# Feed-forward on split operands: the second token chunk's operands made inside the first chunk's product loop, three stage changes with new buffer pools, and the down stage's loads on three queues

## The chip, the core and the metric

The kernel runs on one core of one Trainium2 chip. A core has a matrix engine (TensorE; PE for its matmuls, PEld for its weight loads), VectorE (DVE), ScalarE (ACT), GpSimd (POOL), and SyncE (SP), which here only starts DMAs. Each engine works through its own instruction stream in order. ACT and POOL start DMAs too, and such a start stands in the same stream as their arithmetic. The metric is the device time of one execution in microseconds; lower is better.

## The reference, cut to what matters

With DEPTH = 1 there is one layer: 2-D neighbourhood attention with its residual, then a SwiGLU feed-forward with its residual, then a last norm. The same weights are applied to a prompt of 1024 tokens and a sample of 512 tokens.

```python
D_MODEL = 1024
D_FF = ((8 * D_MODEL // 3 + 255) // 256) * 256      # 2816

def rms_norm(x, g):
    y = xf * lax.rsqrt(jnp.mean(xf * xf, axis=-1, keepdims=True) + RMS_EPS)
    return (y * g.astype(jnp.float32)).astype(x.dtype)

def swiglu(x, w_gate, w_up, w_down):
    return (jax.nn.silu(x @ w_gate) * (x @ w_up)) @ w_down
...
        x = x + neighbourhood_attention(rms_norm(x, norm_mix[i]), ...)
        x = x + swiglu(rms_norm(x, norm_ffn[i]), ffn_w_gate[i], ffn_w_up[i], ffn_w_down[i])
    return rms_norm(x, norm_final)
```

All arrays are float32.

## The kernel before

**Numbers.** Each float32 operand of a matmul is split into a rounded part (a cast to fp32r on ACT, L135) and a remainder (a subtraction on DVE, L136). A product is three matmul passes: high by high, high by low, low by high (`PASS`). `split` does the two steps; ACT goes first and DVE waits for it.

**Feed-forward by seven products.** Gate, up and down are 2 x 2 block products done with seven half-size products in place of eight, so each side needs seven operands, some of which are sums and differences of blocks. The products run in the order 0, 1, 5, 4, 6, 2, 3, and some add to a PSUM bank from which ACT has meanwhile taken a copy (`blocks`, L758 to L783).

**Stages in question.**

1. *Output projection of the attention* (`project`, L575): token tiles of 128 rows. Each half row of x1 goes from the tile `xo` to DRAM (`x1_d`) by a store on POOL (L588).
2. *Norm and operands of the tokens* (`norm2`, L655, and `pair`, L669). The 12 tiles are two chunks of 6. `norm2` loads a tile of x1 (an ACT DMA, L658), forms the norm (square on ACT, power on POOL, multiplication by scale and gain on DVE, L119), transposes it on PE (L665) and copies it out of PSUM (ACT, L666). `pair` joins two tiles into seven operands. The first chunk's go to SBUF (`hops`), the second's to DRAM (`hop_d`) by SP stores (L684), and all six `norm2` of the second chunk are traced before the first product.
3. *Gate and up products* (`unit`, L785): chunk 0 with 11 column steps p, then chunk 1 with 11. A unit is 14 products of 12 matmuls (L751), seven for gate and seven for up. `w_raw` (L706) loads 512 KB of weights at a time on SP, two of five loads into the pool `rpool` that has been open from the start, three of five into `raw2` in the pool `fr`. `w_ops` makes the seven weight operands, tiles `wa`, `ws`, `wt`. The results of a unit go to DRAM as seven operands of the down product (`gop_d`, POOL stores, L802).
4. *Change of chunk* (L807 to L814): the operands of chunk 1 are loaded from `hop_d` in halves `hr` (SP, L812) and split into `hops2`, each into the buffer of chunk 0's operand of the same number.
5. *Down products* (L899 to L934): seven operands n, each with six token tiles tt of 33 matmuls (L907). `d_op` makes 11 weight tiles `wd` from 256 KB loads `dr` (SP, L831; sums on POOL, L845 to L854), `g_op` loads and splits `go` (SP, L861), `x_tile` loads x1 (SP, L873), `finish` norms and stores the result (power on POOL L886, scaling on DVE L889, store on SP, L890).

**What sets the order.** The program is traced in the order of the code. A scheduler then orders each engine's stream by which instruction it expects to be ready, with the trace order as priority. Pools lie in SBUF like two stacks, one from the left and one from the right; a pool opened after another was closed lies over its bytes, and a tile in it waits until the last reader of the bytes under it is done. With `reuse_waits="tile"` that is decided tile by tile.

Of the kernel before, what the change touches and what calls it, by code (L numbers as in the profile page):

```python
# [11 lines left out]
F32 = mybir.dt.float32  # L12
F32R = mybir.dt.float32r
# [42 lines left out]
def body(tc, xp, xs, g_mix, g_ffn, g_fin, w_qkv, rpb, w_o, w_g, w_u, w_d, yp, ys):  # L56
# [9 lines left out]
    with es:  # L66
# [22 lines left out]
        nc.gpsimd.memset(mhalf, -0.5)  # L89

# [539 lines left out]
        hop_cm, hop = pool("hop", bufs=1, reuse_waits="tile")  # L630

        def h_op(i):
            return hop.tile([P, 2, KB // 2, HT], F32R, tag=f"h{i}", name=f"h{i}")

        def operands(dst, xa, xb, tt):

            b11, b21, b12, b22 = xa[:, :4], xa[:, 4:], xb[:, :4], xb[:, 4:]
            t1, t2, t3, t4 = (tt[:, n] for n in range(4))
# [12 lines left out]
        n_cm, np_ = pool("npool", bufs=2, reuse_waits="tile")  # L651
        gb = np_.tile([P, D], F32, name="gbf", bufs=1)
        nc.sync.dma_start(out=gb, in_=bcast(g_ffn))

        def norm2(t):  # L655

            xn = np_.tile([P, D], F32, tag="xn", name="xn", bufs=3)
            nc.scalar.dma_start(out=xn, in_=x1_d[t * P:(t + 1) * P, :])  # L658
            xt = np_.tile([P, KB, P], F32, tag="xt", name="xt")
            rms(xn, gb, xn, xt.rearrange("p k t -> p (k t)"))  # L660
            for b in range(2):
                pt = psum("T", "pt")
                for kk in range(4):
                    k = b * 4 + kk
                    nc.tensor.transpose(pt[:, kk * P:(kk + 1) * P], xn[:, k * P:(k + 1) * P], ident)  # L665
                nc.scalar.copy(xt[:, b * 4:(b + 1) * 4], pt.rearrange("p (k t) -> p k t", k=4))  # L666
            return xt

        def pair(c, j, dst):  # L669
            xa = norm2(c * CT + j)  # L670
            xb = norm2(c * CT + 3 + j)
            tt = np_.tile([P, 4, KB // 2, P], F32, tag="tt", name="tt", bufs=1)
            operands(dst, xa, xb, tt)

        hops = [h_op(i) for i in range(7)]

        def to_sbuf(j):
            def dst(i, op):
                split(op, hops[i][:, 0, :, j * P:(j + 1) * P], hops[i][:, 1, :, j * P:(j + 1) * P])
            return dst  # L680

        def to_dram(j):
            def dst(i, op):
                nc.sync.dma_start(out=hop_d[i, :, :, j * P:(j + 1) * P], in_=op)  # L684
            return dst

        chores = Chores([oh_job(t) for t in range(TP // P - 1, NT)])
        for j in range(3):
            chores.do()
            drain(ofill)  # L690
            pair(0, j, to_sbuf(j))
# [7 lines left out]
        n_cm.__exit__(None, None, None)  # L699
# [3 lines left out]
        fr_cm, fr = pool("fr", bufs=1, side="right", reuse_waits="tile")  # L703
        turn = [0]

        def w_raw(src):  # L706
            turn[0] += 1
            r = rpool.tile([P, 1024], F32, tag="raw", name="wr") if turn[0] % 5 < 2 else \
                fr.tile([P, 1024], F32, tag="raw2", name="wr", bufs=3)
            v = r.rearrange("p (k f) -> p k f", k=KB // 2)  # L710
            nc.sync.dma_start(out=v, in_=src.rearrange("(k p) f -> p k f", p=P))
            return v

        def w_ops(w, p):
# [5 lines left out]
            def one(a):  # L720
                o = fr.tile([P, 2, KB // 2, P], F32R, tag="wa", name="wa", bufs=6)
                split(a, o[:, 0], o[:, 1])
                return lambda z, k: o[:, z, k]

            def two(s):
                o = fr.tile([P, 2, 2, KB // 2, P], F32R, tag="ws", name="ws", bufs=3)
                split(s.rearrange("p s k f -> p (s k f)"), o[:, 0].rearrange("p s k f -> p (s k f)"),
                      o[:, 1].rearrange("p s k f -> p (s k f)"))
                return [lambda z, k, n=n: o[:, z, n, k] for n in range(2)]

            def sums():
                return fr.tile([P, 2, KB // 2, P], F32, tag="wt", name="wt", bufs=3)
# [12 lines left out]
            ops[3] = one(a22)  # L745
# [59 lines left out]
        for p in range(NP):  # L805
            unit(0, p, hops)
        hops2 = [None] * 7  # L807
        for i in (0, 1, 5, 4, 6, 2, 3):
            o = h_op(i)
            for k in range(0, KB // 2, 2):  # L810
                r = fr.tile([P, 2, HT], F32, tag="hr", name="hr", bufs=3)
# [5 lines left out]
        fr_cm.__exit__(None, None, None)  # L817
        fl_cm.__exit__(None, None, None)
        hop_cm.__exit__(None, None, None)
        r_cm.__exit__(None, None, None)  # L820


        dr_cm, drp = pool("drp", bufs=1, side="right", reuse_waits="tile")
        dl_cm, dl = pool("dl", bufs=1, reuse_waits="tile")
        gf = dl.tile([P, D], F32, name="gff")
        nc.sync.dma_start(out=gf, in_=bcast(g_fin))

        def d_raw(i, f, d):
            r = dl.tile([P, 512], F32, tag="dr", name="dr", bufs=6)
            row = (2 * i + f) * P  # L830
            nc.sync.dma_start(out=r, in_=w_d[row:row + P, d * 512:(d + 1) * 512])  # L831
            return r
# [3 lines left out]
        def d_op(n, i):  # L836
# [18 lines left out]
            o = drp.tile([P, 2, 512], F32R, tag="wd", name="wd", bufs=17)  # L855
# [3 lines left out]
        def g_op(n, tt):  # L859
            r = dl.tile([P, NP, P], F32, tag="gr", name="gr", bufs=2)  # L860
# [15 lines left out]
        def finish(t, xs):  # L876
# [10 lines left out]
            for n, (x, y) in enumerate(zip(xs, ys_)):  # L887
                hs = slice(n * 512, (n + 1) * 512)
                nc.vector.scalar_tensor_tensor(y, x, rs, gf[:, hs], ALU.mult, ALU.mult)  # L889
                nc.sync.dma_start(out=yrow(t)[:, hs], in_=y)  # L890
# [8 lines left out]
        for n in (0, 1, 4, 5, 2, 6, 3):  # L899
            wds = [d_op(n, i) for i in range(NP)]  # L900
            for tt in range(6):
# [33 lines left out]
        dl_cm.__exit__(None, None, None)  # L935
        dr_cm.__exit__(None, None, None)
# [17 lines left out]
```

## Time and profile before

| | |
|---|---|
| median of three runs | 1861.57 us (1859.36 to 1862.14) |
| the profiled execution's own time | 1861.16 us |
| its span, first to last instruction | 1859.4 us |
| mean granted TensorE clock | 0.986 |
| PE busy | 1764.7 us, 95% |
| DVE, ACT, POOL busy | 64%, 47%, 24% |
| matmuls of L751 (gate and up) | 3696 |
| matmuls of L907 (down) | 1386 |

Between the span and the profiled execution's own time lie 1.8 us, and between that and the median 0.4 us. PE's matmuls are pipelined, so their listed duration is longer than the step from one to the next; how long PE stood still is read from the idle time in front of a matmul, which the profile gives with what ended it. The stages lie in the span as follows: attention and projection to 812.1 us, gate and up of chunk 0 to 1163.05, of chunk 1 to 1490.44, down products from there to 1851.2, and the last norm and stores to the end.

### The profile page before, as it was taken

To read this page: it belongs to the slowest core of one execution; us is meant where nothing else is said; L and a number is where in the kernel's file an instruction comes from. 1 tells how busy PE (TensorE), PEld (TensorE's weight loads), DVE (VectorE), ACT (ScalarE), POOL (GpSimd) and SP (SyncE) were. 2 spreads that over 40 slices of the span, in tenths; PEclk is the share of its full clock that TensorE was granted. 3 is DMA by queue.
4 is the path that set the end of the run, shared out by engine and by line. 5 is a ranking of instruction groups with operands and counts; after the bars stand their busy time and mean duration, and the time that the engine had idled before them with its cause. 6 is when DMAs were issued, how large, how long until landed. Compare 5 with 4: busy or idle time off the path is not lost.

```text
span 1859.4 us, 25647 instructions
## 1 busy us (share of the span) xinstructions
PE 1764.7 (95%) x9178; PEld 1520.4 (82%) x9178; DVE 1192.7 (64%) x2191; ACT 864.8 (47%) x1706; POOL 447.3 (24%) x494
## 2 busy tenths in 40 slices
PE   8999999999989999988999999999999969999898
PEld 6887777777767777868999999899999958787676
DVE  4401877777886566668777777877777444556554
ACT  4412766666885455544443444544344333333322
POOL 1211000000130000112243342424334224425510
PEclk9999999999999999989999999999999989999999
DMA  7755444333464442776333434534343187545632
GB/s 243 224 176 160 111 111 109 101 102 101 127 203 143 128 145 94 224 242 190 111 119 117 135 113 153 162 118 124 107 131 103 58 304 241 202 133 190 220 122 99
DMA packets 222047, 278.79 MB, mean 150 GB/s; under 512 B 25600, under 2 KB 171776, under 8 KB 221920
## 3 DMA queue, kind: packets, MB, share of 16 engines
q1 hardware_dynamic: 201824, 210.69, 37.6%
q0 software_dynamic: 18368, 60.18, 9.5%
q10 hardware_dynamic: 1728, 6.29, 1.1%
q8 instruction: 72, 1.18, 0.3%
q14 instruction: 55, 0.45, 0.1%
HBM read 213.20 MB, written 76.43 MB: 156 GB/s over the span
## 4 chain that ended last, share of the span: by engine, by line
PE 67%; DVE 11%; DMA 10%; ACT 6%; issue 3%; SPq 2%; POOL 2%; DVEq 0%; POOLq 0%; ACTq 0%
PE pa L751 19%; PE pd L907 13%; PE pd L751 9%; PE pgv L275 7%; DMA vr<-v_d 5%; PE pg L329 5%; PE pb L751 5%; PE pgo L583 4%; DVE pT L421 2%; SPq L375 2%; DMA dr<-ffn_w_down 1%; ACT s L402 1%; PE pss L391 1%; PE ptt L417 1%; PE po L428 1%
## 5 line engine op out<-in xcount | busy, mean ns | idle before, releaser
L907 PE MATMUL pd<-wd,go 128*128 128x512 f32 x1386 | 331.0, 400 | 29.8 <-ACT go L135 19.3
L907 PEld LDWEIGHTS pd<-wd,go 128*128 128x128 f32 x1386 | 262.4, 190 | 98.3 <-ACT go L135 20.3
L751 PE MATMUL pa<-h,ws 128*128 128x384 f32 x1056 | 201.5, 340 | 2.8 <-ACT c L774 2.0
L751 PE MATMUL pa<-h,wa 128*128 128x384 f32 x1056 | 194.1, 339 | 7.4 <-ACT wa L135 5.1
L751 PE MATMUL pd<-h,ws 128*128 128x384 f32 x1056 | 198.6, 337 | 1.5 <-ACT h L135 0.9
L329 PE MATMUL pg<-hTp,whl 128*128 128x512 f32 x768 | 197.0, 403 | 0.0
L751 PEld LDWEIGHTS pa<-h,wa 128*128 128x128 f32 x1056 | 184.9, 190 | 9.2 <-ACT wa L135 5.6
L751 PEld LDWEIGHTS pa<-h,ws 128*128 128x128 f32 x1056 | 184.6, 190 | 6.7 <-ACT c L774 5.3
L136 DVE TENSOR_TENSOR ws<-wt,ws 128x1024 fp32r<-128x1024 f32 x88 | 108.5, 1234 | 126.5 <-ACT ws L135 126.3
L751 PEld LDWEIGHTS pd<-h,ws 128*128 128x128 f32 x1056 | 184.7, 188 | 2.1 <-ACT h L135 1.2
L329 PEld LDWEIGHTS pg<-hTp,whl 128*128 128x128 f32 x768 | 140.2, 189 | 29.8 <-issue 0.4
L802 POOL DMA_DIRECT2D gop_d<-c x66 | 50.5, 765 | 386.9 <-DVE c L793 379.7
L402 ACT ACTIVATE s<-s,mx 128x384 f32<-128x384 f32 (+1 forms) x192 | 110.7, 580 | 66.5 <-DVE mx L399 66.2
L583 PE MATMUL pgo<-wo,oh 128*128 128x512 f32 x576 | 139.3, 392 | 0.0
L136 DVE TENSOR_TENSOR wa<-wr,wa 128x512 fp32r<-128x512 f32 x132 | 117.9, 897 | 18.8 <-ACT wa L135 18.2
L135 ACT CAST ws<-wt 128x1024 fp32r<-128x1024 f32 x88 | 92.5, 1052 | 68.5 <-PE pd L751 65.3
L583 PEld LDWEIGHTS pgo<-wo,oh 128*128 128x128 f32 x576 | 105.5, 188 | 20.6 <-DVE oh L136 0.3
L135 ACT CAST go<-gr 128x1408 fp32r<-128x1408 f32 x42 | 57.7, 1373 | 138.4 <-PE pd L907 116.7
L135 ACT CAST wa<-wr 128x512 fp32r<-128x512 f32 x132 | 81.4, 621 | 63.3 <-PE pb L751 40.0
L751 PE MATMUL pb<-h,wa 128*128 128x384 f32 x528 | 101.8, 342 | 3.6 <-DVE c L771 3.6
L421 DVE TENSOR_TENSOR pT<-ptt,pT 128x384 fp32r<-128x384 f32 (+1 forms) x192 | 90.0, 507 | 21.2 <-ACT pT L420 20.5
L329 PE MATMUL pg<-hTs,whl 128*128 128x512 f32 x384 | 102.6, 404 | 0.8 <-DVE q L340 0.8
(137 smaller groups left out, 2859.0 us busy)
## 6 DMA issues: line engine op xcount, KB each, us to landing
gr<-gop_d SPq DMA_DIRECT2D x42, 704.0 KB
dr<-ffn_w_down SPq DMA_DIRECT2D x99, 256.0 KB
wr<-ffn_w_gate SPq DMA_DIRECT2D x44, 512.0 KB
wr<-ffn_w_up SPq DMA_DIRECT2D x44, 512.0 KB
wr<-na_w_qkv SPq DMA_DIRECT2D x38, 512.0 KB
gop_d<-gs POOLq DMA_DIRECT2D x88, 192.0 KB, 4.3
gop_d<-c POOLq DMA_DIRECT2D x66, 192.0 KB, 2.8
vr<-v_d SPq DMA_DIRECT2D x192, 64.0 KB
```

The lines of the kernel that those rows point to most:

```text
L135: nc.scalar.copy(hi, raw)
L136: nc.vector.tensor_tensor(lo, raw, f32(hi), ALU.subtract)
L275: nc.tensor.matmul(pg, hh[a][:, k, c:c + P], wv[k // 2][b][:, k % 2], start=(k == 0 and i == 0), stop=(k == KB - 1 and i == 2))
L329: nc.tensor.matmul(pg, w[:, a, k, :], h[b][:, k, c:c + 512], start=(k == 0 and i == 0), stop=(k == KB - 1 and i == 2))
L375: nc.sync.dma_start(out=raw[:, j * P:(j + 1) * P], in_=src[:, BS[j]:BS[j] + 32, :])
L391: nc.tensor.matmul(pt[:, :n], q[h * HD:(h + 1) * HD, a, j].rearrange("p r i -> p (r i)"), kv[:, krow:krow + nrow, BS[j]:BS[j] + 32], start ...
L402: nc.scalar.activation(s[:, :n], s[:, :n], AF.Exp, bias=mx, scale=-1.0, accum_out=sm)
L421: nc.vector.tensor_tensor(pT[:, :n, 1], pv, f32(pT[:, :n, 0]), ALU.subtract)
L583: nc.tensor.matmul(pg, ohs[k // 4][:, a, k % 4], wo[:, b, k, n * 512:(n + 1) * 512], start=(k == 0 and i == 0), stop=(k == KB - 1 and i == 2))
L751: nc.tensor.matmul(bank[:, :HT], a(y, k), b[:, z, k], start=start and k == 0 and i == 0, stop=k == KB // 2 - 1 and i == 2, skip_group_chec ...
L802: nc.gpsimd.dma_start(out=gop_d[i, 3 * c:3 * c + 3, :, p].rearrange("j q t -> q j t"), in_=a.rearrange("q (j t) -> q j t", j=3))
L907: nc.tensor.matmul(pd, go[:, y, i], wds[i][:, z], start=(i == 0 and m == 0), stop=(i == NP - 1 and m == 2))
```

## The change

The second chunk's operands are made between the first chunk's units, `pair1` behind units 2, 4 and 6. The gain of the norm, a broadcast tile of 512 KB (`gb`), becomes a tile `gT` with one column for each block of 128 features, loaded at the start of the kernel, and is multiplied in where the transposed tile leaves PSUM: that copy moves from ACT to DVE, and the scaling of the row from DVE to ACT. Chunk 0's operands lie in `hop` in the order of use, so the reload of chunk 1 goes one buffer down: operand number n in the order goes where number n - 1 lay, and the first goes to a pool of its own, `hx`, traced ahead of the last unit. The weight operand tiles move from the right stack to the left (`fa`, over the closed norm pool) and are fewer: `wa` 6 before, now 2 in `fa` and 2 for the last operand in `a2p`; `ws` and `wt` 3 before, now 2 each. The reload's halves and `pair1`'s tiles share four 4 KB buffers (`t4p`); `pair1`'s x1 tiles take turns with the weight loads in `raw2`.

In the down stage `wd` lies left, the `gr`, `dr` and `go` buffers right. `dr` has 4 buffers where it had 6, `go` one in each of two pools, `g1p` first. The load of `gr` goes to ACT's queue, x1 loads and the first half of the result's stores to POOL's, and `dr` loads and the other stores stay on SP.

```diff
+        gT = cpool.tile([P, KB], F32, name="gT")
+        nc.sync.dma_start(out=gT, in_=g_ffn.rearrange("(k p) -> p k", p=P))
...
+        ORDER = (0, 1, 5, 4, 6, 2, 3)
...
-        def norm2(t):
+        def norm2(t, xn, xt):
...
-            rms(xn, gb, xn, xt.rearrange("p k t -> p (k t)"))
+            nc.scalar.activation(xt.rearrange("p k t -> p (k t)"), xn, AF.Square, accum_out=ms)
...
+            nc.gpsimd.tensor_tensor(rs, me, mhalf, ALU.pow)
+            nc.scalar.mul(xn, xn, rs)
...
-                nc.scalar.copy(xt[:, b * 4:(b + 1) * 4], pt.rearrange("p (k t) -> p k t", k=4))
+                nc.vector.tensor_tensor(xt[:, ks], pt.rearrange("p (k t) -> p k t", k=4),
+                                        gT[:, ks].rearrange("p (k o) -> p k o", o=1).to_broadcast([P, 4, P]),
+                                        ALU.mult)
...
+        n_cm.__exit__(None, None, None)
+        fa_cm, fa = pool("fa", bufs=2, reuse_waits="tile")
...
-        for j in range(3):
-            pair(1, j, to_dram(j))
...
-        fr_cm, fr = pool("fr", bufs=1, side="right", reuse_waits="tile")
+        t4_cm, t4p = pool("t4p", bufs=4, side="right", reuse_waits="tile")
+        r2_cm, r2p = pool("r2p", bufs=3, side="right", reuse_waits="tile")
+        a2_cm, a2p = pool("a2p", bufs=2, side="right", reuse_waits="tile")
+        hx_cm, hx = pool("hx", bufs=1, side="right", reuse_waits="tile")
...
+        def pair1(j):
+            xs = []
+            for t in (CT + j, CT + 3 + j):
+                xn = r2p.tile([P, 1024], F32, tag="raw2", name="xn")
+                xt = temp().rearrange("p (k t) -> p k t", k=KB)
+                norm2(t, xn, xt)
+                xs.append(xt)
+            tt = [temp().rearrange("p (s k t) -> p s k t", s=2, k=KB // 2) for _ in range(2)]
+
+            def dst(i, op):
+                nc.sync.dma_start(out=hop_d[i, :, :, j * P:(j + 1) * P], in_=op)
+            operands(dst, *xs, [tt[n // 2][:, n % 2] for n in range(4)])
...
+        def reload(n):
+
+            i = ORDER[n]
+            o = h_op(n - 1) if n else h_op("x", hx)
+            for k in range(0, KB // 2, 2):
+                r = temp()[:, :2 * HT].rearrange("p (k t) -> p k t", k=2)
+                nc.sync.dma_start(out=r, in_=hop_d[i, :, k:k + 2])
+                split(r, o[:, 0, k:k + 2], o[:, 1, k:k + 2])
+            hops2[i] = o
+
+        for p in range(NP):
+            unit(0, p, hops)
+            if p in (2, 4, 6):
+                pair1(p // 2 - 1)
+            if p == NP - 2:
+                reload(0)
+        for n in range(1, 7):
+            reload(n)
...
-        dr_cm, drp = pool("drp", bufs=1, side="right", reuse_waits="tile")
+        gr_cm, grp = pool("grp", bufs=2, side="right", reuse_waits="tile")
+        g0_cm, g0p = pool("g0p", bufs=1, side="right", reuse_waits="tile")
+        dr_cm, drp = pool("drp", bufs=4, side="right", reuse_waits="tile")
+        g1_cm, g1p = pool("g1p", bufs=1, side="right", reuse_waits="tile")
+        wd_cm, wdp = pool("wdp", bufs=17, reuse_waits="tile")
         dl_cm, dl = pool("dl", bufs=1, reuse_waits="tile")
+        turn = [0]
...
-            nc.sync.dma_start(out=r, in_=gop_d[n, tt])
-            o = dl.tile([P, 2, NP, P], F32R, tag="go", name="go", bufs=2)
+            nc.scalar.dma_start(out=r, in_=gop_d[n, tt])
+            turn[0] += 1
+            o = (g0p, g1p)[turn[0] % 2].tile([P, 2, NP, P], F32R, tag="go", name="go")
...
-            nc.sync.dma_start(out=x, in_=x1_d[t * P:(t + 1) * P, d * 512:(d + 1) * 512])
+            nc.gpsimd.dma_start(out=x, in_=x1_d[t * P:(t + 1) * P, d * 512:(d + 1) * 512])
...
-                nc.sync.dma_start(out=yrow(t)[:, hs], in_=y)
+                queue.dma_start(out=yrow(t)[:, hs], in_=y)
...
-                    finish(rows(tt, 0), (c11[tt], c12[tt]))
+                    finish(rows(tt, 0), (c11[tt], c12[tt]), nc.gpsimd)
...
-                    finish(rows(tt, 1), (u2[tt], c22[tt]))
+                    finish(rows(tt, 1), (u2[tt], c22[tt]), nc.sync)
```

More of the change, by code (lines that the diff above doesn't have):

```diff
@@ L630, in body, with h_op @@
         hop_cm, hop = pool("hop", bufs=1, reuse_waits="tile")
-        def h_op(i):
-            return hop.tile([P, 2, KB // 2, HT], F32R, tag=f"h{i}", name=f"h{i}")
+        ORDER = (0, 1, 5, 4, 6, 2, 3)
+        def h_op(n, where=None):
+            return (where or hop).tile([P, 2, KB // 2, HT], F32R, tag=f"h{n}", name=f"h{n}")
         def operands(dst, xa, xb, tt):
             b11, b21, b12, b22 = xa[:, :4], xa[:, 4:], xb[:, :4], xb[:, 4:]
-            t1, t2, t3, t4 = (tt[:, n] for n in range(4))
+            t1, t2, t3, t4 = tt
             dst(0, b11)
@@ L718, in w_ops, with one @@
             a11, a21, a12, a22 = d1[:, :, :P], d1[:, :, P:], d2[:, :, :P], d2[:, :, P:]
-            def one(a):
-                o = fr.tile([P, 2, KB // 2, P], F32R, tag="wa", name="wa", bufs=6)
+            def one(a, where=fa):
+                o = where.tile([P, 2, KB // 2, P], F32R, tag="wa", name="wa")
                 split(a, o[:, 0], o[:, 1])
@@ L744, in w_ops @@
             ops[6], ops[2] = two(r)
-            ops[3] = one(a22)
+            ops[3] = one(a22, a2p)
             return ops
@@ L828, in d_raw @@
         def d_raw(i, f, d):
-            r = dl.tile([P, 512], F32, tag="dr", name="dr", bufs=6)
+            r = drp.tile([P, 512], F32, tag="dr", name="dr")
             row = (2 * i + f) * P
```

64 lines of the change are left out of this document (29 added, 35 removed).

## The prediction

> **What bounds the kernel now.** The page's span and chain come first.
>
> ```profile
> span 1859.4 us, 25647 instructions
> ...
> PE 67%; DVE 11%; DMA 10%; ACT 6%; issue 3%; SPq 2%; POOL 2%; DVEq 0%; POOLq 0%; ACTq 0%
> ```
>
> The chain that ends last is mostly PE, so a change pays only where PE stands still. The view of busy time by stretches, cut at the stage changes, tells where that is. Columns: start:end, length, PE, PEld, DVE, ACT, POOL busy (instructions), granted clock, DMA share, GB/s.
>
> ```profile
> 812.10:863.10 51.00, 36.33 (x176) 32.97 (x175) 35.65 (x53) 25.30 (x43) 3.69 (x5) 0.80 0.84 260
> 863.10:1163.05 299.95, 299.95 (x1724) 297.85 (x1723) 225.95 (x297) 129.11 (x213) 107.36 (x112) 1.00 0.42 126
> 1163.05:1181.50 18.45, 13.90 (x74) 12.43 (x74) 15.46 (x19) 11.39 (x18) 9.27 (x9) 1.00 0.79 250
> 1181.50:1490.44 308.94, 308.93 (x1775) 307.18 (x1775) 214.92 (x284) 123.28 (x204) 107.39 (x113) 1.00 0.35 106
> 1490.44:1508.73 18.29, 1.22 (x2) 0.50 (x2) 10.06 (x13) 8.78 (x13) 6.88 (x9) 0.59 0.95 341
> 1508.73:1689.80 181.07, 180.75 (x769) 144.95 (x770) 88.04 (x85) 59.43 (x74) 63.34 (x41) 0.99 0.60 203
> 1689.80:1772.90 83.10, 70.65 (x289) 54.20 (x287) 55.28 (x60) 30.60 (x51) 44.09 (x32) 0.98 0.67 218
> 1772.90:1851.20 78.30, 78.30 (x328) 62.71 (x328) 35.04 (x44) 20.01 (x33) 7.80 (x8) 0.98 0.31 108
> ```
>
> Inside the units PE is full; it stands still at the three stage changes and in one stretch of the down stage. What a stage would take without stalls comes from the chain in order of time (the same point of two units, nine units apart) and the DVE timeline (PSUM read after two successive tiles).
>
> ```profile
> 1196.16 4.16 PE pa L751 x24
> ...
> 1459.23 4.16 PE pa L751 x24
> ```
>
> ```profile
> 1789.67 0.69 DVE L893 TENSOR_TENSOR c<-c,pd 128x512 f32<-128x512 f32 x1 [4.67 <-PE pd L907]
> ...
> 1797.37 0.69 DVE L893 TENSOR_TENSOR c<-c,pd 128x512 f32<-128x512 f32 x1 [4.66 <-PE pd L907]
> ```
>
> A unit takes 263.07 / 9 = 29.23 us, 11 units 321.5; a down tile 7.70, 42 tiles 323.4. The ledger: chunk 0 takes 350.95 (812.10 to 1163.05), 29.4 too much. Chunk 1 takes 327.4, 5.9 too much. The down products take 360.8 (1490.44 to 1851.20), 37.4 too much: 17.8 before they run, 83.10 - 289/33 x 7.70 = 15.7 in the stretch from 1689.80, and 3.9 elsewhere.
>
> **First change, 812 us.** PE and ACT timelines, SP timeline, a stretch, and two groups:
>
> ```profile
> 819.36 3.33 PE L751 MATMUL pa<-h,wa 128*128 128x384 f32 x9 [4.91 <-ACT wa L135]
> 825.72 1.94 PE L665 MATMUL pt<-ident,xn 128*128 128x128 f32 x8 [3.03 <-DVE xn L119]
> ```
>
> ```profile
> 818.69 0.62 ACT L135 CAST wa<-wr 128x512 fp32r<-128x512 f32 x1 [3.56 <-DMA x_d<-xo]
> ...
> 822.48 1.14 ACT L135 CAST wa<-wr 128x512 fp32r<-128x512 f32 x2 [0.28 <-DMA wr<-ffn_w_gate]
> ```
>
> ```profile
> 814.66 1.47 SPq L711 DMA_DIRECT2D wr<-ffn_w_gate  x1
> ```
>
> ```profile
> 820.20:832.00 11.80, 8.77 (x32) 8.26 (x32) 8.14 (x12) 5.54 (x9) 1.42 (x2) 0.52 1.03 321
> ```
>
> ```profile
> L119 DVE SCALAR_TENSOR_TENSOR xn<-xn,rs,gbf 128x1024 f32<-128x1024 f32 x12 | 15.4, 1285 | 8.4 <-POOL rs L116 8.4
> L665 PE MATMUL pt<-ident,xn 128*128 128x128 f32 x96 | 13.7, 289 | 4.1 <-DVE xn L119 3.7 <-ACT xt L666 0.3
> L666 ACT COPY xt<-pt 128x512 f32<-128x512 f32 x24 | 13.0, 591 | 17.4 <-PE pt L665 17.4
> ```
>
> The first `wa` lies over the projection's `xo` and waits for its store (3.56). The change puts `wa` over the norm pool, done before 812, so product 0 can follow the projection at once. The second load still lies over `wo`, read to 812.1; its operands are late next. A 512 KB load took 4.56 us in an empty pipe (x at the start, below) and 7.8 here beside stores (814.66 to 822.48). With 0.62 for the cast and less the 2.08 of product 0 (half of the 4.16 for 24 matmuls), PE waits 3.1 to 6.4; I take 3.5, near the empty pipe, since the stores of the second chunk are gone from there. The half clock (0.52 for 11.8 us) behind a wait of 4.91 cost up to 5.7; I take 2.5. The transposes stay PE work, at most 13.7 / 2 = 6.9, so 29.4 - 6.9 = 22.5 is stall, and **16.5** goes (10.4 to 19.4). The Trainium skill, "TensorE: Matmul & The Clock Gate", Part 1, states that an idle window of some 3.4 us throttles the array; the row with 4.91 agrees; by it, 3.1 of idle would keep the clock and the sum gains 2.5.
>
> The norm itself: per tile ACT gives two copies of 0.591 for one full-width scaling (the nearest row, DVE's, is 1.285), DVE gives 1.285 for two PSUM reads of 0.69. That is nothing on PE. In the units DVE is 75% busy (225.95 of 299.95), which hides it; without that cover it would be about 1.4 us a tile.
>
> **The second chunk among the units.** Each `norm2` puts an ACT DMA that waits for a `raw2` buffer, two ACT passes, and PE transposes that wait for them into full streams; behind the ACT wait stand PSUM copies that PE needs; behind the seven SP stores of a pair, weight loads, which run ahead. Nothing shows this; the nearest row is the transposes' 3.03. Six tiles cost 0 to 18.2; I take 0.7 each, because the DMA share is 0.42 there and was 1.03 around that row: **-4**.
>
> **Second change, 1163 us.** PE timeline, ACT timeline, group:
>
> ```profile
> 1173.49 2.36 PE L751 MATMUL pa<-h,ws 128*128 128x384 f32 x12 [1.96 <-ACT c L774]
> ```
>
> ```profile
> 1176.93 0.83 ACT L135 CAST h<-hr 128x768 fp32r<-128x768 f32 x1 [3.11 <-DMA hr<-hop_d]
> ```
>
> ```profile
> L136 DVE TENSOR_TENSOR h<-hr,h 128x768 fp32r<-128x768 f32 x14 | 14.2, 1025 | 4.8 <-ACT h L135 4.8
> ```
>
> One buffer down gives each operand one product (2.08 us) more, and operand 0 (2 x 1.025 of DVE) goes ahead. Twelve halves are still 12.3 us of DVE within two blocks in which it is mostly busy. Of 5.9 I take **3.5** (0 to 5.9).
>
> **Third change, 1490 us.** SP's waits; PE, ACT, DVE timeline:
>
> ```profile
> SPq L831 <- PE pa L751: 51.3, 1, 51.3
> ```
>
> ```profile
> 1505.65 1.36 ACT L135 CAST go<-gr 128x1408 fp32r<-128x1408 f32 x1 [1.14 <-DMA gr<-gop_d]
> 1507.05 1.63 DVE L136 TENSOR_TENSOR go<-gr,go 128x1408 fp32r<-128x1408 f32 x1 [1.82 <-ACT go L135]
> ...
> 1507.07 1.22 PE L907 MATMUL pd<-wd,go 128*128 128x512 f32 x2 [16.64 <-ACT go L135]
> ```
>
> SP waits 51.3 us for the last product, since `dr` lies over its operand; then come 11 loads, then `gr`. In the new layout `wd` 0 to 10 lie over `rpool` and operands used early in the last block, `dr` and `gr` over closed temporaries: all can be there at the end. What is late next is `go`: `g1p`, taken first, lies over `a2p`, which the last product reads. PE then waits 1.36 + 1.63 and a little, 3.2; I add 1 for late `wd`. 17.8 - 4.2 = **13.6** goes (0 to 14.6; 0 if SP, in order, is held by the load of `gff`, which now lies over that last operand).
>
> **Fourth, 1690 to 1773 us.** SP's and PE's waits in this stretch, the one after it, and a group:
>
> ```profile
> SPq L890 <- DVE yo L889: 30.3, 12, 6.4
> ```
>
> ```profile
> PE pd L907 <- DVE go L136: 9.7, 6, 4.1
> ```
>
> ```profile
> 1772.90:1782.00 9.10, 9.10 (x32) 7.25 (x33) 2.70 (x4) 0.03 (x1) 5.05 (x3) 0.81 0.48 159
> ```
>
> ```profile
> L802 POOL DMA_DIRECT2D gop_d<-gs x88 | 67.3, 767 | 0.1
> ```
>
> SP stands 30.3 us before result stores, with `dr` loads queued behind; weights come late and hold ACT, DVE, and `go`. The stores go to POOL, which here works 44.09 of 83.10; 12 stores and 6 x1 loads add 18 x 0.767 = 13.8, and behind each store's wait for L889 stand the weight sums for the next operand. The `gr` loads now wait in ACT's stream for DVE's remainder of an earlier tile, in front of `wd` casts; ACT, busy 30.60 of 83.10, has room for that. And `dr` has 4 buffers, not 6. So I take half of 15.7 and 1 of the clock's 3.9 (0.81 after the last wait): **9** (-5 to 19.6). The Trainium skill, "DMA: Bandwidth & Descriptors", section "Issuing engines are not separate DMA queues", states that issuing from several engines saves only sequencer time; the DMA share of 0.67 does not contradict it, but SP's 30.3 us show that order can matter.
>
> **Start.** Timelines of SP and ACT:
>
> ```profile
> 0.74 0.38 SPq L246 DMA_DIRECT2D x<-x_prompt  x1
> ...
> 5.30 1.06 ACT L112 ACTIVATE xn<-x 128x1024 f32<-128x1024 f32 x1 [3.28 <-DMA x<-x_prompt]
> ...
> 18.55 3.98 SPq L305 DMA_DIRECT2D t_d<-na_rpb  x6
> ```
>
> `gT` is traced before the first x load, on which everything waits: 1024 pieces of 4 bytes. A table load of 240 pieces takes SP 3.98 / 6 = 0.66; by pieces that is 2.8. I take **-3** (0 to -5).
>
> **Sum:** 16.5 - 4 + 3.5 + 13.6 + 9 - 3 = 35.6 less than the profiled execution's 1861.2, which is 0.4 under the median: **1826 us**. All good ends give 1802, all bad ones 1879.
>
> **Rivals.**
> - *The down stage starts late as before* (SP held by `gff`, or `gr` by the last `gop_d` stores). For it: SP's 51.3 us wait. Against: SP's timeline shows weight loads (L711) started 23 us ahead of stores traced earlier (L684), so what isn't ready need not hold the rest.
>
> ```profile
> 790.02 0.38 SPq L711 DMA_DIRECT2D wr<-ffn_w_gate  x1
> ...
> 813.28 1.27 SPq L684 DMA_DIRECT2D hop_d<-xt  x2
> ```
>
>   1826 + 13.6 = 1840. Chance 0.12.
> - *Other queues win nothing in the fourth stretch*: either transfers share engines, as the page says, or POOL becomes what SP was. 1826 + 9 = 1835, to 1840. Chance 0.15; it lies inside the range.
> - *Slower:* the units lose. A copy on ACT must be done within one product:
>
> ```profile
> 1025.21 2.03 PEld L751 LDWEIGHTS pa<-h,ws 128*128 128x128 f32 x12 [0.16 <-ACT c L774]
> ```
>
>   There is 0.16 us of stall already. With `ws` 2 and `wa` 2 + 2, a cast that waits for a product in front of that copy holds PE. From 35.6 / 22 = 1.6 us a unit the gain is gone; at 2 us the time is 1870. Against: by the code a `ws` buffer is read last by the fourth of seven products and needed again by the third of the next seven, five products or 10.4 us on. Chance 0.13.
> - *Nothing in sum:* the stalls move, 1861. Chance 0.05.
>
> **Chances and range.** My forecast has 0.55 (1808 to 1842). The range 1808 to 1852 leaves out the slower rival, the null and tails, 0.2. A measurement tells 0.2%, 3.7 us, from no change: faster 0.81, same 0.05, slower 0.14.
>
> **What would show it.** First change: `wa` cast before 812, one PE wait of 3 to 6 us. Units: L751 with some 4 us of idle; over 20 speaks for the slower rival. 1163: under 3 us. Third: L907 starts within 5 us of the last L751. Fourth: no SP wait before stores, and POOL's own waits for DVE `yo` under 15 us. First ACT square near 8.3 us rather than 5.30. I am wrong if unit periods exceed 30 us, or if L907 starts 15 us late.

## The result and the profile after

| | before | after |
|---|---|---|
| median of four runs each, one chip | 1860.46 us (1856.5 to 1862.14) | 1874.99 us (1874.36 to 1877.8) |
| ratio, 95% interval | | 1.0082 (1.0065 to 1.01) |
| the profiled execution's own time, its span | 1861.16, 1859.4 us | 1877.8, 1875.7 us |
| chunk 0 of gate and up (321.5 us without stalls) | 350.95 | 359.7 |
| chunk 1 (321.5) | 327.4 | 326.0 |
| down products (323.4) | 360.8 | 369.7 |

The change makes the kernel slower by 14.5 us. The prediction said 1826 us, 1808 to 1852; the time lies above the range, on the slower side, which had a chance of 0.14.

Lines have moved: L751 is now L775, L907 is L945, `dr` loads L868, `gr` L898, x1 loads L911, powers L664 and L924, weight sums of the down stage L882 to L891. The view of busy time by stretches of the changed kernel, cut as the prediction's was (start:end, length, PE, PEld, DVE, ACT, POOL busy, clock, DMA share, GB/s):

```profile
812.70:845.42 32.72, 29.18 (x157) 28.54 (x156) 22.81 (x34) 15.50 (x24) 1.31 (x2) 0.95 0.52 159
845.42:1172.39 326.97, 307.76 (x1742) 301.77 (x1741) 232.43 (x321) 141.26 (x229) 107.79 (x117) 0.98 0.47 145
1172.39:1190.00 17.61, 16.07 (x90) 15.43 (x90) 16.55 (x20) 10.04 (x18) 9.78 (x9) 1.00 0.83 280
1190.00:1498.40 308.40, 307.22 (x1760) 306.13 (x1759) 220.13 (x288) 124.29 (x205) 107.18 (x113) 1.00 0.36 110
1498.40:1531.70 33.30, 21.53 (x69) 15.30 (x69) 13.83 (x17) 11.70 (x17) 17.94 (x27) 0.85 0.92 317
1531.70:1726.50 194.80, 188.51 (x790) 150.21 (x790) 95.01 (x92) 59.50 (x75) 75.43 (x49) 0.98 0.52 173
1726.50:1791.17 64.67, 52.38 (x201) 39.97 (x200) 36.17 (x46) 24.23 (x43) 37.66 (x39) 0.92 0.69 227
1791.17:1868.10 76.93, 76.93 (x328) 61.41 (x328) 40.08 (x47) 21.37 (x34) 11.69 (x10) 1.00 0.34 115
```

Compare it with the table of before. PE was full from 863 to 1163 us, with not one stall inside the units; now it stands still for 326.97 - 307.76 = 19.2 us there and runs at a lower clock behind the longer waits. The start of the down stage still has a hole, and so has the stretch in which the first half of the result is finished. The first boundary is what did come out. PE timeline:

```profile
817.87 0.62 PE L775 MATMUL pb<-h,wa 128*128 128x384 f32 x2 [2.93 <-ACT wa L137]
819.09 3.01 PE L775 MATMUL pb<-h,wa 128*128 128x384 f32 x10 [0.60 <-DVE wa L138]
```

Two waits of 2.93 and 0.60 us stand where there was a stall of 22.5. By 845.42 the matmuls are 5.6 us behind an unbroken stream.

**Where the time went.** Chunk 0 lasts 8.7 us longer (the units lost more than the boundary gained), chunk 1 is 1.4 shorter, the down stage 8.9 longer; with 0.6 more before and 0.6 less behind, that is the 16.3 us between the spans. Code that is the same everywhere spreads as well: the projection ends between 806.9 and 812.7 us in the profiles of this study, and chunk 0 with unchanged code took 355 to 360.5 us. So what follows compares stages, and takes the timed ratios for the whole.

**In the units.** The largest of PE's waits and of SP's from 812 to 1173 us (total, times, longest), then the timelines of SP, ACT, POOL, ACT and PE before the longest wait:

```profile
PE pa L775 <- ACT c L793: 7.3, 3, 4.7
PE pa L775 <- ACT c L798: 5.9, 4, 4.9
PE pb L775 <- ACT wa L137: 5.2, 3, 2.9
PE pd L775 <- ACT c L801: 2.3, 2, 1.6
```

```profile
SPq L735 <- DVE wa L138: 186.0, 27, 17.3
SPq L735 <- PE pt L671: 41.1, 3, 22.0
SPq L735 <- DVE me L662: 22.0, 1, 22.0
```

```profile
911.39 8.99 SPq L727 DMA_DIRECT2D hop_d<-t  x7
920.47 2.64 SPq L735 DMA_DIRECT2D wr<-ffn_w_gate  x2
```

```profile
942.26 1.06 ACT L660 ACTIVATE t<-xn 128x1024 f32<-128x1024 f32 x1 [0.50 <-DMA xn<-x_d]
```

```profile
945.22 1.92 POOL L821 TENSOR_TENSOR gs<-c 128x384 f32<-128x384 f32 x1 [0.66 <-DVE c L817]
...
955.11 1.08 POOL L664 TENSOR_TENSOR rs<-me,mhalf 128x1 f32<-128x1 f32 x2
```

```profile
955.71 1.15 ACT L665 ACTIVATE xn<-xn,rs 128x1024 f32<-128x1024 f32 x1 [5.37 <-POOL rs L664]
...
958.22 0.46 ACT L798 COPY c<-pa 128x384 f32<-128x384 f32 x1
```

```profile
958.73 4.21 PE L775 MATMUL pa<-h,ws 128*128 128x384 f32 x12 [4.88 <-ACT c L798]
```

Read from the bottom: PE waits for ACT's copy of a PSUM bank. In ACT's stream the scaling of `xn` stands before that copy and waits for the power; POOL reaches the power only at 955.11, behind a unit's sums and stores. It is so late because the tile's x1 came late (squares at 940 to 943). The rows of SP's waits explain more than this one wait: for 41.1 + 22.0 us SP's weight loads wait for a transpose (L671) or a statistic (L662) of the pair. The pair's two x1 tiles take turns in the three `raw2` buffers, and the weights that should be loaded there, and SP's queue behind them, wait until `xn` is read.

### The profile page after: what moved, and what is told of

The parts are those of the page before. It is cut to its first block, busy times and chain, and to the rows that moved or that the text cites. A ratio compares the mean times of both kernels' runs of the same rounds, so it can differ in the third digit from the quotient of the medians.

```text
span 1875.7 us, 25644 instructions
## 1 busy us (share of the span) xinstructions
PE 1775.9 (95%) x9178; PEld 1528.7 (82%) x9178; DVE 1187.4 (63%) x2203; ACT 863.8 (46%) x1694; POOL 466.7 (25%) x530
## 5 line engine op out<-in xcount | busy, mean ns | idle before, releaser
L945 PE MATMUL pd<-wd,go 128*128 128x512 f32 x1386 | 339.3, 406 | 30.3 <-DVE go L138 13.2
L945 PEld LDWEIGHTS pd<-wd,go 128*128 128x128 f32 x1386 | 266.9, 194 | 102.7 <-DVE go L138 16.8
L775 PE MATMUL pa<-h,ws 128*128 128x384 f32 x1056 | 202.7, 340 | 16.4 <-ACT c L798 8.4
L775 PEld LDWEIGHTS pa<-h,ws 128*128 128x128 f32 x1056 | 186.5, 191 | 20.7 <-ACT c L798 10.3
L775 PE MATMUL pd<-h,ws 128*128 128x384 f32 x1056 | 198.4, 335 | 2.3 <-ACT c L801 2.3
L775 PEld LDWEIGHTS pd<-h,ws 128*128 128x128 f32 x1056 | 184.9, 188 | 3.0 <-ACT c L801 3.0
L775 PE MATMUL pa<-h,wa 128*128 128x384 f32 x792 | 149.2, 338 | 0.8 <-DVE c L803 0.8
L775 PEld LDWEIGHTS pa<-h,wa 128*128 128x128 f32 x792 | 139.4, 188 | 1.9 <-DVE c L803 1.8
L775 PE MATMUL pb<-h,wa 128*128 128x384 f32 x528 | 100.8, 338 | 6.0 <-ACT wa L137 5.2
```

What stands on the lines that cost most here:

```text
L775: nc.tensor.matmul(bank[:, :HT], a(y, k), b[:, z, k], start=start and k == 0 and i == 0, stop=k == KB // 2 - 1 and i == 2, skip_group_chec ...
L945: nc.tensor.matmul(pd, go[:, y, i], wds[i][:, z], start=(i == 0 and m == 0), stop=(i == NP - 1 and m == 2))
```

## The experiments

"Against before" is the difference of the medians on the same chip, with the ratio's interval; the changed kernel itself stands at +14.5 us (1.0065 to 1.01). "Loss" is the length of a stage less its time without stalls. Each diff is against the changed kernel unless said otherwise.

**1. The `dr` buffers off the last product's operand.** By the built program's addresses the first `dr` buffer lies at 194 to 196 KB of each partition, inside `a2p`'s second buffer (192 to 196 KB), which holds the operand of the very last gate and up product. Opened ahead of `g0p`, `dr` lies at 205 to 213 KB.

```diff
-        g0_cm, g0p = pool("g0p", bufs=1, ...)
         dr_cm, drp = pool("drp", bufs=4, ...)
+        g0_cm, g0p = pool("g0p", bufs=1, ...)
```

> Changed kernel with the pools of dr and of the second go tile opened in the other order, so that the four dr buffers lie over weight-load and temporary bytes that are free before the last product. Theory (the dr loads, in order on SP, are held by the buffer that the last product reads): loads start before the last product ends, the start of the down stage loses 5 to 8 us in place of 17.2, and the time falls by 9 to 13, to 1862 to 1866. Rival (the start is bound by the go tile over the same kind of buffer, or by the 11 casts themselves): the loss stays above 14 and the time within 3 of 1875.

Measured: 1867.75 us, 8.8 against before (1.0032 to 1.0065). SP's queue (timeline), the changed kernel first, then this run:

```profile
1498.45 5.47 SPq L868 DMA_DIRECT2D dr<-ffn_w_down  x5
```

```profile
1467.50 28.95 SPq L868 DMA_DIRECT2D dr<-ffn_w_down  x8
```

The first `dr` load starts 22.6 us ahead of the end of gate and up (1490.12 here) where it started behind it (1498.40), after 25.5 us of waiting for PE (L775). The stage has lost 13.0 us up to the 39th matmul where it had lost 15.2 up to the 41st. So the held buffer was real, but freeing it gives 5.7 us, about half of the 9 to 13, and the start itself still loses 13 where 5 to 8 were expected.

**2. All pairs in front of the units.**

```diff
+        for j in range(3):
+            pair1(j)
         for p in range(NP):
             unit(0, p, hops)
-            if p in (2, 4, 6):
-                pair1(p // 2 - 1)
```

> Changed kernel with the three pairs of the second chunk traced ahead of the first unit, all else (pools, buffers, reload of operand 0 before the last unit) as in it. Theory (the stalls among the units come from the pairs' work standing in front of c copies on ACT and in the weight loads' way): units 2 to 10 of chunk 0 lose some 8 in place of 28, the first boundary gets back some 16, so the time falls by some 8, to about 1867. Rival (the stalls come from two wa, ws and wt buffers instead of six and three): the 28 stay, the boundary costs its 16 as well, and the time is about 1891.

Measured: 1869.29 us, 10.3 against before (1.004 to 1.0071). Its stretches in chunk 0:

```profile
808.22:846.00 37.78, 16.59 (x73) 13.61 (x72) 18.29 (x33) 16.60 (x23) 4.22 (x7) 0.59 0.76 226
846.00:1163.88 317.88, 317.88 (x1827) 316.78 (x1825) 243.26 (x323) 141.39 (x230) 106.41 (x112) 1.00 0.44 139
```

From 846 us PE is full, with the same two `wa`, `ws` and `wt` buffers: the rival of fewer buffers falls. The stalls belong to the pairs among the units. Moving them out paid 34.2 us of loss at the boundary in place of 38.2 in all of chunk 0. Even the reload of operand 0 costs nothing here.

**3, 4. The queues, or the four `dr` buffers.** Run 3 puts `gr`, x1 loads and all result stores back on SP; run 4 leaves the queues and gives `dr` six buffers.

```diff
-            nc.scalar.dma_start(out=r, in_=gop_d[n, tt])
+            nc.sync.dma_start(out=r, in_=gop_d[n, tt])
...
-            nc.gpsimd.dma_start(out=x, in_=x1_d[...])
+            nc.sync.dma_start(out=x, in_=x1_d[...])
...
-                    finish(rows(tt, 0), (c11[tt], c12[tt]), nc.gpsimd)
+                    finish(rows(tt, 0), (c11[tt], c12[tt]), nc.sync)
```

> Changed kernel with the loads of gr, the x1 loads of the down stage and all result stores back on SP. Theory A (ACT is held in order by the gr load's own wait, POOL by x1 loads and stores): the 8.2 us lost at 1578 to 1625 and the 17.8 at 1727 to 1791 fall to some 2 and 15, the time by 6 to 9, to 1866 to 1869. Theory B (four dr buffers in place of six do it): the losses stay or grow, as SP has more to hold it, and the time is 1873 to 1880.

> Changed kernel with six dr buffers in place of four; the first four of them then lie over bytes free before the last product, only the fifth and sixth over the last product's operand. Theory B (four buffers throttle the sums on POOL and the casts): the losses at 1578 to 1625 and 1727 to 1791 fall together by 8 or more, and the start loses some 10 in place of 17.2: time 1857 to 1862. Theory A (the queues): the start alone gains, 5 to 8 us: 1867 to 1870.

Measured: queues back 1859.28 us, 0.3 against before (0.9993 to 1.0012); six buffers 1868.36 us, 9.4 against before (1.0035 to 1.0065). The three queues cost 14 us, twice what was expected of them, and the buffers 5. How the loss of the down stage grows, from the PE timeline (start of the row, less the stage's start, less the matmuls before it times 323.4 / 1386):

| loss in us up to | before | after | queues back | six `dr` | gr back (run 5) | x1, stores back (run 9) |
|---|---|---|---|---|---|---|
| about the 70th of 1386 matmuls | 17.8 | 17.4 | 9.8 | 8.5 | 17.4 | 10.4 |
| operand 4, third tile (the 432nd) | 19.4 | 26.1 | 16.1 | 11.8 | 25.3 | 19.7 |
| the last stall | 35.6 | 45.9 | 28.4 | 37.4 | 39.4 | 36.5 |

Two things gain at the start, each about 8. Between there and operand 4 the changed kernel loses 8.7 where the kernel before lost 1.6; with six buffers that is 3.3, with the queues back 6.3. In the last stretch it loses 19.8; with the queues back 12.3, and with six buffers 25.6, so that part of what six buffers gain ahead is lost again there.

**5, 9, 10. Which queue.** `gr` alone back on SP; x1 loads and stores back; stores alone back.

> Changed kernel with the gr loads alone back on SP; x1 loads and the first half of the result's stores stay on POOL. The loads and stores together, put back on SP, gave 15.6 us. Theory A1 (it is ACT, held in order by the gr load's wait for its buffer, that starves the casts): this part gives 10 or more, time 1859 to 1865. Theory A2 (it is POOL, held by x1 loads and result stores, so that dr sums and powers come late): this gives 4 or less, time 1871 to 1875.

> Changed kernel with the x1 loads and the first half of the result's stores of the down stage back on SP; gr alone stays on ACT. With gr alone back the time fell by 5, with all three by 15.6. If the parts add, this gives 10 to 11, time some 1864. If each hides the other, so that only both together help, it gives 5 or less, time 1870 or more.

> Changed kernel with only the result's stores of the first half back on SP; x1 loads stay on POOL, gr on ACT. If POOL is held by the store's wait for the scaled row (6.7 us in five waits of the trace), the stretch at operand 2 loses 4 or more less and the time is 1871 or less. If it is the issue of the x1 loads and the waits behind them, the time stays within 2 of 1875.

Measured against before: `gr` back +11.2 (1.003 to 1.0076), x1 loads and stores back +7.5 (1.0019 to 1.005), stores alone back +12.9 (1.0045 to 1.0088). So `gr` on ACT costs some 3 (theory A2's case), the stores some 2 and the x1 loads some 5 (the difference of the last two), each uncertain by about 4 us; together that is 10 of the 14 of run 3. Run 9 falls between its two cases; run 10, with 1870.76 us, meets its first by the time and its second by the difference (1.6 us gained). The trace shows how x1 loads hurt at the start. POOL timeline of the changed kernel:

```profile
1506.01 0.58 POOL L911 DMA_DIRECT2D c<-x_d  x1
1513.39 3.21 POOL L911 DMA_DIRECT2D c<-x_d  x6 [6.79 <-issue]
1516.59 0.54 POOL L911 DMA_DIRECT2D x<-x_d  x1
```

Fifteen of the 24 x1 loads start before 1526 us, most for tiles that are wanted over 100 us later, while the first weights are on the way (DMA share 0.92). On SP the same loads stand among the `dr` loads: in the same 27.6 us of the stage 7 start in runs 3 and 9. The loss at the start goes with them: 17.4 and 18.7 in runs 5 and 10, which leave them on POOL, 9.8 and 10.4 in runs 3 and 9. That they take bandwidth from `dr` is read from these rows and not tried by itself.

**6, 8. Where the pairs' cost comes from.** Run 6 gives the x1 tiles of `pair1` two buffers of their own, in bytes that `hx` uses only later, and traces load, square and power one unit ahead. Run 8 gives the buffers alone.

```diff
-        hx_cm, hx = pool("hx", bufs=1, ...)
+        xq_cm, xq = pool("xq", bufs=2, ...)
...
-                xn = r2p.tile([P, 1024], F32, tag="raw2", name="xn")
+                xn = xq.tile([P, 1024], F32, tag="xq", name="xn")
...
             if p == NP - 2:
+                xq_cm.__exit__(None, None, None)
+                hx_cm, hx = pool("hx", bufs=1, ...)
                 reload(0)
```

> Changed kernel with pair1 cut in two: load, square and power are traced behind units 1, 3 and 5, scaling, transposes and operands behind units 2, 4 and 6; the x1 tiles lie in two buffers of their own (in the bytes of hx, which is opened at the reload) and no longer among the weight loads. Theory (scaling on ACT waits for the power that stands behind the unit's sums on POOL, and the x1 tiles take weight buffers): the 4.9 us wait and the slow product behind it go, and the waits for wa near the first pair shrink: 8 to 11 us less, 1864 to 1867. Rival (it is the amount of work that pairs bring to ACT, DVE and SP, wherever it stands): the stalls move and the time stays within 3 of 1875.

> Changed kernel in which only the x1 tiles of pair1 get two buffers of their own in the bytes of hx; pair1 stands whole where it stood. With the norm part traced a unit ahead as well, chunk 0 had lost 17 us less. Theory (what costs is the scaling on ACT behind the power, which stands behind the sums on POOL): the wait of 4.9 us and the slow product behind it stay, and this part gives at most 6, time 1869 or more. Rival (what costs is that x1 tiles take two of the three raw2 buffers, so that weights, weight operands and all behind them come late): it gives 12 or more, time 1863 or less.

Measured: both 1858.02 us, -1.2 against before (0.9984 to 1.0009); buffers alone 1857.32 us, -0.5 (0.9987 to 1.0008). My theory falls: tracing ahead adds nothing that can be told from noise, the buffers are all of it. PE's waits from 846 to 1145 us with buffers alone, complete, the two largest of SP's queue from 812 to 1173, and POOL's powers:

```profile
PE pa L775 <- ACT c L793: 3.9, 1, 3.9
PE pa L775 <- ACT c L798: 2.0, 2, 1.3
```

```profile
SPq L735 <- DVE wa L138: 211.6, 36, 15.3
SPq L727 <- DVE t L672: 36.6, 6, 11.0
```

```profile
914.81 0.56 POOL L664 TENSOR_TENSOR rs<-me,mhalf 128x1 f32<-128x1 f32 x1 [2.18 <-DVE me L662]
916.22 0.56 POOL L664 TENSOR_TENSOR rs<-me,mhalf 128x1 f32<-128x1 f32 x1 [0.84 <-DVE me L662]
```

No weight load waits for a transpose any more, and the powers of the second pair come 107.2 us after the chunk's start (807.57) and not 142.4 (812.70), ahead of the unit's sums on POOL instead of behind them. Chunk 0 takes 344.2 us: 15.5 less than in the changed kernel, 6.7 less than before. Most of what the prediction wanted of the interleaving is there once the weights' buffers are left alone: its terms would have left a loss of 29.4 - 16.5 + 4 = 16.9 in this chunk, and 22.7 remain.

**7. The reload later.** The one long wait left (3.9; 4.7 in the changed kernel) belongs to the casts of `hx`, which stand in front of a copy and wait for `hop_d`. In this run of the changed kernel the two loads come behind the last weight load traced before them (an ordering edge on SP).

> Changed kernel in which SP starts the two loads of operand 0 of the second chunk only behind the last weight load traced before them, where the scheduler had drawn them up behind the last hop_d stores. Theory (the casts of hx, drawn up with them, hold ACT until the data is there): the waits of 4 us in front of a c copy in unit 8 and the slow product behind go, 5 to 8 us less, 1867 to 1870. Rival (the casts stand in front of another copy and wait as long there, or come late for the second chunk): within 2 of 1875 or above.

Measured: 1874.67 us, 15.5 against before (1.006 to 1.0108): nothing. The wait has moved to another copy, the rival's case. PE timeline:

```profile
1088.02 3.92 PE L775 MATMUL pd<-h,ws 128*128 128x384 f32 x12 [4.21 <-ACT c L801]
```

**11, 12. Together.** First queues back, six `dr` buffers, the pairs' own buffers with the norm ahead, and the late reload; then the same without the late reload.

> Changed kernel with four of these edits together: gr, x1 loads and result stores on SP, six dr buffers, the norm part traced a unit ahead in its own buffers, the reload behind the weight loads. If the causes are separate, their gains add but for the start of the down stage, which two of them share: 15.6 + 2 + 9 + 6, time some 1842, under the kernel before by 16. If each stall only gives its place to the next, the time stays at or above 1852.

> Changed kernel with three edits: queues as before, six dr buffers, the norm part a unit ahead in buffers of its own; the reload where the changed kernel has it. If the late reload is worth nothing, as its run alone said, the time is that of the four edits, 1835 to 1840. If it was only covered there by the pairs' stalls, this is 4 or more longer.

Measured: 1837.05 us, -22.2 against before (0.9854 to 0.9908); 1834.54 us, -23.3 (0.986 to 0.9894). The gains add: the queues, the six buffers and the pairs' own buffers with the norm ahead gave 14.2, 5.1 and 15.7 us singly and 37.8 together. The reload is worth nothing again. The down stage now starts with its first matmul in the stream and loses 4.6 us up to the seventh, but the last stretch still goes from 8.5 to 20.5. PE timeline of the three-edit kernel, where L945 has become L959:

```profile
1745.30 78.35 PE L959 MATMUL pd<-wd,go 128*128 128x512 f32 x328 [4.04 <-DVE go L138]
```

**13, 14, 15. The last stretch.** In the changed kernel SP waits for no store there, as planned, and it loses more. Waits of all engines from 1726 to 1792 us:

```profile
ACT yo L919 <- DVE c L931: 17.8, 4, 8.1
DVE yo L927 <- POOL rs L924: 14.9, 5, 6.7
```

The timelines of POOL, DVE and PE at the longest of these waits, then ACT and PE of the kernel before:

```profile
1742.05 1.29 POOL L966 TENSOR_TENSOR c<-c,u 128x512 f32<-128x512 f32 x1 [3.85 <-DMA c<-x_d]
1743.30 1.29 POOL L891 TENSOR_TENSOR dr<-dr 128x512 f32<-128x512 f32 x1
...
1745.77 0.56 POOL L924 TENSOR_TENSOR rs<-me,mhalf 128x1 f32<-128x1 f32 x1
```

```profile
1746.36 1.41 DVE L927 SCALAR_TENSOR_TENSOR yo<-c,rs,gff 128x512 f32<-128x512 f32 x2 [6.62 <-POOL rs L924]
...
1748.29 1.62 DVE L138 TENSOR_TENSOR go<-gr,go 128x1408 fp32r<-128x1408 f32 x1
```

```profile
1749.96 24.85 PE L945 MATMUL pd<-wd,go 128*128 128x512 f32 x94 [5.36 <-DVE go L138]
```

```profile
1755.73 0.62 ACT L135 CAST wd<-tk 128x512 fp32r<-128x512 f32 x1 [5.42 <-POOL tk L845]
```

```profile
1757.66 0.73 PE L907 MATMUL pd<-wd,go 128*128 128x512 f32 x2 [2.62 <-ACT go L135]
```

The chain of the changed kernel reads: POOL's power stands behind weight sums that wait for `dr` and behind an addition (L966) that waits 3.85 us for an x1 load; DVE's scaling waits for the power, and behind the scaling stand the next addition into `c` and the remainder of `go`, for which PE waits. ACT's next square waits for that addition, and later casts of `go` stand behind it. In the kernel before there is a second way from the sums to PE: a cast of `wd` on ACT waits 5.42 us for a sum, and the cast of `go` stands behind it. To try whether the sums are the cause, the sums of operands 6 and 3 go to DVE, in the changed kernel, in the three-edit kernel, and in the kernel before with its own queues.

```diff
-                nc.gpsimd.tensor_tensor(b, d_raw(i, 1, 0), b, ALU.subtract)
+                nc.vector.tensor_tensor(b, d_raw(i, 1, 0), b, ALU.subtract)
...
-                nc.gpsimd.tensor_tensor(b, b, d_raw(i, 0, 1), ALU.subtract)
+                nc.vector.tensor_tensor(b, b, d_raw(i, 0, 1), ALU.subtract)
```

> Changed kernel with the weight sums of operands 6 and 3 on DVE in place of POOL (22 subtractions). Theory (the power of the last norm stands on POOL behind sums that wait for dr; the scaling on DVE, the squares on ACT and the go casts behind them follow): DVE's wait for the power, 14.9 us, falls under 5, the stretch loses some 8 in place of 16, time some 1867. Rival (the weights themselves come late, four buffers and x1 loads in the way): the sums hold DVE in place of POOL and the stretch loses 16 or more, time 1873 or above.

> The three-edit kernel (queues as before, six dr buffers, norm part a unit ahead in its own buffers) with the weight sums of operands 6 and 3 on DVE in place of POOL. Theory (POOL's order): DVE's wait for the power falls from 16.6 to under 5, the stretch's loss from 12 to some 5, time 1827 to 1830. Rival (supply of weights, or DVE now the engine that is late): the loss stays above 10, time 1833 or more.

> The kernel before, with the weight sums of operands 6 and 3 of the down products on DVE in place of POOL, and SP's queue as it was. If SP's waits in front of result stores make the loss of 15.7 us from 1690 to 1773, as the prediction had it, they stay and the time stays within 4 of 1858. If it is the norm's power, in POOL's order behind weight sums that wait for their loads, the loss falls to 5 or less and the time by 9 to 14, to 1844 to 1849.

Measured: changed kernel 1866.25 us, 8.6 against before (1.0029 to 1.0057), so 6 gained; three edits and sums **1816.96 us, -40.7** (0.9752 to 0.9799), 17 below the three edits; the kernel before with the sums 1842.64 us, -15.7 (0.9894 to 0.9931). Stretches, three edits and sums first, then the kernel before with the sums, then SP's waits in the latter from 1680 to 1790 us:

```profile
1690.00:1760.00 70.00, 70.00 (x301) 56.31 (x300) 49.55 (x69) 25.93 (x39) 6.81 (x8) 1.00 0.63 215
```

```profile
1689.80:1760.00 70.20, 70.20 (x303) 56.55 (x302) 56.38 (x78) 30.71 (x52) 13.27 (x12) 1.00 0.81 267
```

```profile
SPq L890 <- DVE yo L889: 17.6, 11, 4.4
```

PE is full in both. In the kernel before, SP still waits 17.6 us for stores, and nothing is lost by it. So the sums on POOL are the cause there. By which way is not shown: the power comes earlier without them, but so do the casts of `wd`. A sum takes 0.68 us on DVE and 1.29 to 1.73 on POOL (medians), so speed and order moved together as well; which counts more was not separated. DVE's wait for the power fell to 8.0 us in run 13 and 9.6 in run 14, not under 5: it is harmless at that size rather than gone. With four `dr` buffers and the x1 loads on POOL (run 13) the stage still loses 13.8 from the 432nd matmul on, where it lost 19.8; DVE's 7.9 and ACT's 5.5 us of waits for `dr` between 1670 and 1800 us point to the supply of weights, which was not tried there by itself.

## Why the prediction failed, by its own steps

- **First change, 16.5: right.** A cast of `wa` at 800.39, waits of PE of 2.93 and 0.60 us for 3.5, 5.6 us left where 6 was forecast. The clock was the smaller half, as taken. That the sum agrees so closely is in part luck: in run 8 the same wait is 4.25 us and 7.9 are left. On the rule cited there (the Trainium skill, "TensorE: Matmul & The Clock Gate", Part 1), the trace speaks against the reading that 3.1 us of idle keeps the clock: behind the 2.93 and 0.60 the ten matmuls took 3.01 us where ten took 1.89 in a full stream.
- **Second chunk among the units, -4: this is the step that failed most.** Chunk 0 lost 38.2 us, of which 5.6 stand at the boundary and 4.7 are the transposes (in the PE timeline the 16 of a pair push the matmuls back by 0.79, 0.41 and 0.36 us); 28 are stalls. The text named the x1 load that waits for a `raw2` buffer and priced it by its wait on PE. It did not ask the reverse: what waits for the buffer while x1 sits in it. That was the weight loads, 63 us of SP's queue. With buffers of their own the pairs leave 22.7 of loss in the whole chunk, of which some 10 are stalls among the units.
- **The slower rival** had the place right (an ACT copy that must be done within one product is held) and the wrong cause: two `ws` and `wa` buffers stall nothing (run 2). It gave 1870, the time was 1875.
- **Second change, 3.5:** measured 1.4 (4.5 left). The mechanism was right; the c12 copy still waits 1.35 us.
- **Third change, 13.6: failed.** Loss 17.4 for 17.8. L945 did start 3.5 us behind the last L775, as its sign asked, but the term that allowed 1 us for late `wd` was far too small: 13.9 more are lost up to the 69th matmul, 7.7 of them in waits for `wd` (the longest 4.11 us) and most of the rest at a lower granted clock (0.85 in that stretch). "`dr` over closed temporaries" was false: stacks and sizes put the first `dr` buffer on the last operand, and with it SP in order. That was the rival "starts late as before", by another tile than it named. Moving `dr` alone takes some 2 to 3 us from the start; the start falls to 4.6 only with six buffers and the queues back.
- **Fourth, 9: failed, and its reason with it.** The 15.7 was put down to SP's 30.3 us before stores. Run 15 takes the loss away with the order of SP's queue as it was: 17.6 of the 30.3 us of waits remain, and nothing is lost by them; whether the 12.7 that went were a link of the chain is not shown. What made the loss were the weight sums on POOL, worth 15.7. The prediction's own caveat (weight sums behind POOL's stores) pointed at the right engine; the rival "POOL becomes what SP was" had 0.15 and was priced at no loss, where three queues cost 14. On the section cited there (the Trainium skill, "DMA: Bandwidth & Descriptors", "Issuing engines are not separate DMA queues"): the rows agree that nothing is gained by issuing from more engines. They show beside it that something can be lost. No term of the prediction stood for the stretch up to operand 4, where 7.1 of the 8.9 us by which the down stage grew were lost.
- **Start, -3:** the first square came at 5.46 us for 5.30, and SP spent 0.43 us on `gT`; the term was nearly nothing.

Of the 35.6 us hoped for, 18.3 came at the two boundaries (16.9 and 1.4). The units' stalls took 28 where 4 were allowed, and the down stage grew by 8.9 where a gain of 22.6 was hoped for.

## What to carry to other kernels

When work is moved into a full stream, list whose buffers it borrows and ask what waits for them meanwhile, not only what it waits for itself; a shared ring of load buffers passes every delay to the queue behind. When a load is taken out of a shared in-order queue, it also loses its place behind more urgent loads and may run far ahead. And a long wait of a queue is a cause only when what stands behind it is late: SP's waits before stores looked like the cause of the last stretch, and moving 22 subtractions off POOL ended the loss while 17.6 us of those waits stayed. Behind such subtractions stand tiny instructions (a power of 128 numbers) for which other engines wait.

## What the runs showed of the hardware

This is about the clock behind a wait of PE in the units. In all profiles, for twelve matmuls (2.24 us in a full stream): behind waits of 1.1 to 2.1 us they took 2.35 to 2.75 us (over 50 cases); behind waits of 3.6 to 4.9 us always 3.2 to 4.2 (21 cases). Between them it went both ways: 2.27 and 3.02 us were followed by 3.87 and 3.79, 2.73 and 3.06 by 2.36 and 2.38. The granted clock in two such stretches of the changed kernel:

```profile
958.73:962.95 4.22, 4.22 (x13) 4.22 (x14) 1.23 (x1) 1.27 (x2) 0.00 (x0) 0.50 0.05 18
...
1182.27:1184.50 2.23, 2.23 (x13) 2.23 (x14) 2.23 (x5) 0.35 (x1) 0.39 (x1) 1.00 1.02 221
```

So a wait of 4 us costs nearly 6 in all, one of 2 us little more than itself. That the border is not sharp fits what the Trainium skill says ("TensorE: Matmul & The Clock Gate", Part 1), that the window of activity runs freely. The drop behind 2.27 us (granted clock 0.57 in run 11) does not fit the idle window of some 3.4 us that it gives, and there the measurement decides.
